# Gate and up projections by seven half-size products (Strassen's scheme) in a tuned trunk layer

## The chip, the cores and the metric

The kernel runs on one core of one Trainium2 chip. Its time is the device time of one execution in microseconds; a kernel is run three times and the median is given. One further execution is recorded by the hardware profiler, and every row below comes from that one.

## The reference, cut to what matters

One inference step of one trunk layer for 512 prompt tokens and 8 sequences of 4 sample tokens, 544 tokens in all, model width 1024. A mixing sub-layer (convolutions, short convolution, dilated attention, an output projection) is followed by a channel sub-layer, a gated MLP of inner width 2816. The part that the change touches is the second one:

```
    h = _rmsnorm(x, lp['g_pre_ffn']) * (1 + sc_f) + sh_f
    g, new_f = _causal_dwconv(h @ lp['w_gate'], st_f, lp['conv_f_w'])
    f = jax.nn.silu(g) * (h @ lp['w_up'])
    x = x + ga_f * _rmsnorm(f @ lp['w_down'], lp['g_post_ffn'])
```

`_causal_dwconv` is a convolution over three tokens for each channel. Everything is float32; `sc_f`, `sh_f` and `ga_f` come from a small projection of a conditioning vector (weights `ada`), one value for the whole prompt and one for each sample sequence.

## The kernel before

Tokens lie on the free axis in two halves of H = 272 (`h` 0 and 1; the sample tokens are the last 32 of half 1), channels on 128 partitions in chunks: the model width is 8 chunks, the inner width 22 blocks of 128. A float32 product is three passes (`mm3`, L231 to L233): weights and activations are each split into a high part that the TensorE takes as fp32r and the low rest, and high·high, high·low and low·high are added up in PSUM. One block of 128 outputs for one half is 8 chunks × 3 passes = 24 matmuls of 272 columns.

Splitting weights is `prep`: ScalarE copies 1024 columns of raw weights into the high part (L227), VectorE or GpSimd subtracts to get the low part (L228). Raw weights come by SyncE's DMA queue into a ring of four slots of 1 MB (`Ring`); a slot is refilled when its last user is done. Split weights go round in three sets of tiles, `st[0..2]` (`sth`/`stl`).

The instructions of each engine stand in the order in which the program's steps are written; engines wait for each other by semaphores. Three pieces of the program matter here.

The string `FLOW` orders the stretch from the out-projection to the first three gate/up pairs. In it `a` and `b` are steps of the chain `post_mix` for half 0 and half 1 (norm, residual, second norm, and `modul`, which makes the MLP's input `z` as `zh`/`zl`); `m` is a gate or up product, `y` and `u` its evaluations `gate_ev` and `up_ev`, `g` a weight split, `d0` to `d3` four steps of the `ada` projection (`adb_step`, L309), `f` their end. A p at the end of a name puts the work on GpSimd, else it is VectorE's.

Then the loop over pairs: for each inner block `j` from 3 to 21 the gate product for both halves, its evaluation (PSUM to SBUF on ScalarE, three taps on VectorE, Silu on ScalarE), the up product for both halves, its evaluation (product with the gate, split of the result `f` into `fh`/`fl` for the down projection), and two weight splits for the next pair:

```
    for j in range(NA, NFF):
        for h in range(2):
            step(lambda j=j, h=h: gu_mm(2 * j, h))
        step(lambda j=j: gate_ev(j, 0))
        gu_or_dn_prep(2 * j + 3)
        step(lambda j=j: gate_ev(j, 1))
```

Then the down projection: units of 8 chunks of its weights, split by `dn_prep` one after the other into the three sets, and `dn_mm`.

The factor of a norm is worked out on few partitions and spread over 128 by `rs_bc`: three matmuls of float32 against the identity for each half (L266).

Of the kernel before, what the change touches and what calls it, by code (L numbers as in the profile page):

```python
# [13 lines left out]
F32 = mybir.dt.float32  # L14
# [6 lines left out]
T = NP + NB * NT  # L21
# [23 lines left out]
         "02 12 P3d2 22 03 H3 A4 31 30 32 Q2p4 H4 13 23 33 A5 40123 H5 A6 A7 501 52 H6 H7 P4d2 53 6012 701 Q4p4 63 "  # L45
         "723")
FLOW = ("p3d w1068 w0068 w2008 e10 w3008 e20 p4d p6p p5d w4008 e00 e40 p7d w5008 e50 w6008 w7008 w7104 e30 e60 e70 "
        "a w7148 e71 a a a a w2108 w1108 a e11 w3108 e21 a w4104 a g0p e31 p0d a w4148 g1p a a a e41 a a w5108 e51 "
        "a w6108 a a a e61 o w0108 g2d e01 m0004 b g3d x m0048 b m1003 d0 g4p b b d1 b b m1038 m2008 b g5d m3008 b "
        "b d2 b b b d3 b b b b b m4008 b y10 y00 m5008 f u10 m0108 g6d m1108 m2107 m2178 y20 u00 g7p y01 u01 u20 "  # L50
        "m4108 m3108 y11 m5108 y21 u11 g8d u21")

_V = {}
_n = 0
# [42 lines left out]
def body(tc, nc, A):  # L97
# [75 lines left out]
    class Ring:  # L173


        def __init__(self):
            self.slots, self.free, self.order, self.pos, self.uses, self.where = {}, [], [], 0, {}, {}

        def setup(self):
            for _, keys in plan:  # L180
# [33 lines left out]
        def done(self, k):  # L214
            self.uses[k] -= 1
            if not self.uses[k]:
                self.free.append(self.where.pop(k))
                self.pump()

    ring = Ring()  # L220

# [5 lines left out]
            act.activation(hi, r[:, a:a + n, :], AF.Copy)  # L227
            eng.tensor_sub(lo, r[:, a:a + n, :], hi.bitcast(F32))  # L228

    def mm3(acc, wh, wl, rh, rl, start, stop):  # L230
        pe.matmul(acc, wh, rh, start=start, stop=False)  # L231
        pe.matmul(acc, wh, rl, start=False, stop=False)  # L232
        pe.matmul(acc, wl, rh, start=False, stop=stop)  # L233

    ALL = tuple(range(NCH))

# [2 lines left out]
        for c in cs:  # L239
            mm3(acc[:, :H], pair[0][:, c, :], pair[1][:, c, :], a[h][:, c, :], b[h][:, c, :], c == first, c == last)  # L240

    BLK = ((0, 128, 0), (128, 128, 0), (256, H - 256, 384 - H))

    def rs_acc(parts, tsum, nh, first, last):

        for j, s in enumerate(parts):
            for h in range(nh):
                for i, o in enumerate((0, 128, H - 128)):
                    pe.matmul(tsum[:, 3 * h + i:3 * h + i + 1], s[:, h * H + o:h * H + o + 128], ones[:, 0:1],  # L249
                              start=first and j == h == i == 0, stop=last and j == len(parts) - 1,  # L250
                              skip_group_check=True)
# [10 lines left out]
    def rs_bc(r, outs):  # L262

        for h, o in enumerate(outs):
            for i, (c0, n, k0) in enumerate(BLK):
                pe.matmul(o[:, c0:c0 + n], r[:, 3 * h + i:3 * h + i + 1].to_broadcast([128, 128]),  # L266
                          idn[:, k0:k0 + n], start=True, stop=True)

    class Banks:

# [647 lines left out]

    Q = {}
    p2r = ExitStack()  # L920
    p2l = ExitStack()
    x2s = ExitStack()

    def open_p2():
        p1.close()
        psc.close()
        p = psc.enter_context(tc.tile_pool(name="psd", bufs=1, space=bass.MemoryType.PSUM))
        Q["sc"] = [p.tile([128, 512], F32, name=f"sc{i}") for i in range(2)]
        x2p = x2s.enter_context(tc.tile_pool(name="x2p", bufs=1, side="right"))
        Q["xh"] = [x2p.tile([128, NCH, H], F32R, name=f"zh{i}") for i in range(2)]  # L930
        Q["xl"] = [x2p.tile([128, NCH, H], F32R, name=f"zl{i}") for i in range(2)]
        xy = p2r.enter_context(tc.tile_pool(name="xyp", bufs=1, side="right"))
        Q["x"] = [xy.tile([128, NCH, H], F32, name=f"x2_{i}") for i in range(2)]
        Q["y"] = [xy.tile([128, NCH, H], F32, name=f"y2_{i}") for i in range(2)]
        Q["tmp"] = xy
        Q["ss"] = [xy.tile([128, 2, H], F32, name=f"ss2_{i}") for i in range(2)]
        Q["rc"] = xy.tile([128, NNEW], F32, name="rc")
        wq = p2l.enter_context(tc.tile_pool(name="p2w", bufs=1))
        Q["w"] = [(wq.tile([128, 8, 128], F32R, name=f"woh{i}"), wq.tile([128, 8, 128], F32R, name=f"wol{i}"))
                  for i in range(4)]  # L940
        for h in range(2):
            pool.dma_start(Q["x"][h], A["x"][:, :, h * H:h * H + H])
        act.activation(Q["rc"][:, 0:1], ones[:, 0:1], AF.Silu)
# [47 lines left out]
    def post_mix(h):  # L991
# [30 lines left out]
        ts_ = {}  # L1022

        def lo(c):
            dve.scalar_tensor_tensor(dl[:, c, :n], ts_.pop(c)[:, :n], sh[:, c, 0:1], dh[:, c, :n].bitcast(F32),
                                     op0=OP.add, op1=OP.subtract)

        def modul(c):
            if c == 0 and h == 1:
# [24 lines left out]
        chains[h].pop(0)()  # L1054

    gu_set = {0: st[2], 1: st[0], 5: st[1]}
    for i in range(6, 2 * NFF):
        gu_set[i] = st[(2, 0, 1)[(i - 6) % 3]]
    dn_set = [st[(2, 0, 1)[(i + 2 * NFF - 6) % 3]] for i in range(64)]

    def gu_prep(i, eng=dve):
        step(lambda: prep(ring.get(("gu", i // 2))[:, (i % 2) * 1024:(i % 2) * 1024 + 1024], gu_set[i], eng),
# [2 lines left out]
    R = {}  # L1065
    p3t = ExitStack()
    p3w = ExitStack()

    def open_p3():
        p2l.close()  # L1070
# [5 lines left out]

    NA = 3

    def f_slices(j, h):
        if j < 8:  # L1080
            return xh[h][:, j, :], xl[h][:, j, :]
        return R["fh"][h][:, j - 8, :], R["fl"][h][:, j - 8, :]


    def gu_mm(i, h, a=0, b=NCH):
        acc = acb.take((i, h)) if a == 0 else bk[acb.of[i, h]]
# [3 lines left out]
        return Q["sc"][1]  # L1090

    def ada_fin():
        adb_end(1, bk_ada(), Q["y"][1][:, 0, :256])
        gain(gqf, 40, "gqf", False)

    G = {}
# [4 lines left out]
    def gate_ev(j, h):  # L1101
# [12 lines left out]
            pool.tensor_copy(fpo[:, j, :], gp[:, NP:])  # L1114
            pool.tensor_copy(fso[:, j, :, :], gs[:, :, NT:])
        n = H if h == 0 else HB
        y = gy()
        G[j, h] = y
        c0 = h * H
        dve.tensor_scalar(y[:, :n], gp[:, c0:c0 + n], V("cfw", 3 * j), None, op0=OP.mult)  # L1120
# [10 lines left out]
    def up_ev(j, h):  # L1131
# [4 lines left out]
        act.activation(fh, y, AF.Copy)  # L1136
        dve.tensor_sub(fl, y, fh.bitcast(F32))

    def close_xy():
        p2r.close()  # L1140
        p3w.close()
        f = p3w.enter_context(tc.tile_pool(name="fp", bufs=1))
        R["fh"] = [f.tile([128, NFF - 8, H], F32R, name=f"fh{i}") for i in range(2)]
        R["fl"] = [f.tile([128, NFF - 8, H], F32R, name=f"fl{i}") for i in range(2)]

    wo_prep(2, pool)
    for fn in late:
# [3 lines left out]
    for w in FLOW.split():  # L1151
        k, i = w[0], [int(c) for c in w[1:] if c.isdigit()]
        eng = pool if w[-1] == "p" else dve
        if k == "p":
            wo_prep(i[0], eng)
        elif k == "w":
            step(lambda i=i: wo_mm(*i))
        elif k == "e":
            step(lambda i=i: wo_ev(*i))
        elif k in "ab":  # L1160
            step(lambda h="ab".index(k): run_chain(h))
        elif k == "g":
            gu_prep(i[0], eng)
        elif k == "m":
            step(lambda i=i: gu_mm(*i))
        elif k == "d":
            s_adc(i[0])
        elif k == "y":
            step(lambda i=i: gate_ev(*i))
        elif k == "u":  # L1170
            step(lambda i=i: up_ev(*i))
        elif k == "f":
            step(ada_fin)
        elif k == "o":
            step(open_p3)
        else:
            step(lambda: ring.add_tiles([Q[k][0].rearrange("p c t -> p (c t)") for k in "xy"], ("adc",)))
    step(close_xy)


# [13 lines left out]
        step(lambda: prep(ring.get(("dn", u // 2))[:, (u % 2) * 1024:(u % 2) * 1024 + 1024], dn_set[i]),  # L1194
             ("dn", u // 2))

    def gu_or_dn_prep(i):
        if i < 2 * NFF:
            gu_prep(i)
        else:  # L1200
            dn_prep(i - 2 * NFF)

    for j in range(NA, NFF):
        for h in range(2):
            step(lambda j=j, h=h: gu_mm(2 * j, h))
        step(lambda j=j: gate_ev(j, 0))
        gu_or_dn_prep(2 * j + 3)
        step(lambda j=j: gate_ev(j, 1))
        for h in range(2):
            step(lambda j=j, h=h: gu_mm(2 * j + 1, h))  # L1210
        step(lambda j=j: up_ev(j, 0))
        gu_or_dn_prep(2 * j + 4)
        step(lambda j=j: up_ev(j, 1))

    def ff_state_out():
        pool.dma_start(A["o_fp"], fpo)
# [2 lines left out]
    step(ff_state_out)  # L1219

    def open_p4():
        x2s.close()
        p = p4.enter_context(tc.tile_pool(name="p4", bufs=1, side="right"))
        S["x"] = [p.tile([128, NCH, H], F32, name=f"x4_{i}") for i in range(2)]
        S["y"] = [p.tile([128, NCH, H], F32, name=f"y4_{i}") for i in range(2)]
        for h in range(2):
            pool.dma_start(S["x"][h], xd[:, :, h * H:h * H + H])
        S["ss"] = [p.tile([128, 2, H], F32, name=f"ss4_{i}", bufs=1) for i in range(2)]
# [8 lines left out]
    def dn_mm(i, u, hs, qs):  # L1237
        for q in qs:
            m, k = MK[q]
            for h in hs:  # L1240
                if k == 0:
                    ACC[m, h] = acb.take((m, h))
                fh, fl = f_slices(k, h)
                mm3(ACC[m, h][:, :H], dn_set[i][0][:, q - 8 * u, :], dn_set[i][1][:, q - 8 * u, :], fh, fl,
                    k == 0, k == NFF - 1)
            if k == NFF - 1:
                for h in hs:
                    acb.give((m, h))
                    post_sq(h, m, m, ACC.pop((m, h)), S["ss"][h], S["y"][h], gqf, gy)

    def gy():
        return R["t"].tile([128, H], F32, name="gy", bufs=3)

    def final(h):

# [39 lines left out]
        for k in keys:  # L1295
            ring.done(k)
    p4.close()
    p3w.close()
    p3t.close()
    psc.close()  # L1300
    ctx.close()


# [102 lines left out]
```

## Time and profile before

| | |
|---|---|
| time, median of 3 runs | 759.72 us (758.55 to 762.98) |
| the profiled execution | 758.35 us, of which its instructions span 756.5 us |
| TensorE (PE) busy | 724.0 us, 96% |
| VectorE (DVE) busy | 438.7 us, 58% |
| ScalarE (ACT) busy | 295.6 us, 39% |
| GpSimd (POOL) busy | 200.3 us, 26% |

Times in the profile count from the first instruction of the span. Busy time is a share over the whole span; the stages below differ from it. A matmul's row shows 0.29 us from issue to end, but matmuls overlap, so the start of one to the start of the next is what a row costs. "Idle before" names what the engine waited for.

### The profile page before, as it was taken

How to read it: one execution, taken by the hardware profiler on the slowest of the kernel's cores; microseconds unless marked ns; L12 is line 12 of the kernel's file. 1: busy time of each engine (PE TensorE's matmuls, PEld its weight loads, DVE VectorE, ACT ScalarE, POOL GpSimd, SP SyncE). 2: the span in 40 equal slices, each digit the busy share in tenths (PEclk: the TensorE clock that was granted, in tenths of full speed). 3: DMA queues.
4: the chain of work that ended last, by engine and by line, in shares of the span. 5: the costliest groups of instructions: out<-in, count | busy, mean ns of one | idle time of the engine just before them, and what ended most of it. 6: DMA issues, size and time to landing. Idle time of an engine off the chain costs nothing.

```text
span 756.5 us, 15327 instructions
## 1 busy us (share of the span) xinstructions
PE 724.0 (96%) x6356; PEld 682.8 (90%) x6356; DVE 438.7 (58%) x879; ACT 295.6 (39%) x632; POOL 200.3 (26%) x254
## 2 busy tenths in 40 slices
PE   8998898979999989989999999999999999999994
PEld 8887776967879789988999999999999999999994
DVE  4869888885354464477767666666556641111343
ACT  4434343635452336553333433333333323222440
POOL 3644232312232255475211011110101110100124
PEclk9999999999999989999999999999999999999997
DMA  9979962766656547058212231312213171220002
GB/s 357 416 265 291 320 253 88 280 236 250 274 221 232 201 163 260 26 186 314 109 66 70 102 113 56 112 63 106 101 68 112 57 240 64 105 71 41 1 29 90
DMA packets 30549, 121.22 MB, mean 160 GB/s; under 512 B 11168, under 2 KB 13488, under 8 KB 21392
## 3 DMA queue, kind: packets, MB, share of 16 engines
q1 hardware_dynamic: 27952, 112.49, 41.0%
q0 software_dynamic: 1808, 7.07, 2.7%
q8 instruction: 50, 0.82, 0.4%
q10 hardware_dynamic: 720, 0.69, 0.3%
q14 instruction: 19, 0.16, 0.1%
HBM read 113.05 MB, written 7.18 MB: 159 GB/s over the span
## 4 chain that ended last, share of the span: by engine, by line
PE 53%; POOL 1%; DVE 1%; ACT 0%; issue 0%; POOLq 0%; DVEq 0%
PE bk L231 17%; PE bk L233 17%; PE bk L232 17%; PE sc L249 1%; PE sc L266 1%; POOL y L1014 0%; DVE y L988 0%; PE sc L309 0%; DVE x L989 0%; POOL y L988 0%; POOL x L989 0%; ACT wgh L227 0%; POOL rr L259 0%; POOLq L1402 0%; DVE y L1014 0%
## 5 line engine op out<-in xcount | busy, mean ns | idle before, releaser
L231 PE MATMUL bk<-zh,sth 128*128 128x272 f32 x656 | 189.6, 289 | 0.0
L233 PE MATMUL bk<-zh,stl 128*128 128x272 f32 x656 | 189.6, 289 | 0.0
L232 PE MATMUL bk<-zl,sth 128*128 128x272 f32 x656 | 188.8, 288 | 0.0
L228 DVE TENSOR_TENSOR stl<-ring,sth 128x1024 fp32r<-128x1024 f32 (+2 forms) x78 | 88.0, 1136 | 152.4 <-ACT sth L227 152.4
L231 PE MATMUL bk<-xh,sth 128*128 128x272 f32 x488 | 146.2, 300 | 2.1 <-DVE q L546 2.1
L233 PE MATMUL bk<-xh,stl 128*128 128x272 f32 x488 | 142.8, 293 | 0.0
L232 PE MATMUL bk<-xl,sth 128*128 128x272 f32 x488 | 142.7, 292 | 0.0
L227 ACT ACTIVATE sth<-ring 128x1024 fp32r<-128x1024 f32 (+3 forms) x104 | 101.9, 991 | 84.9 <-PE bk L232 82.3
L231 PEld LDWEIGHTS bk<-zh,sth 128*128 128x128 f32 x656 | 123.7, 189 | 0.4 <-issue 0.4
L232 PEld LDWEIGHTS bk<-zl,sth 128*128 128x128 f32 x656 | 124.0, 189 | 0.0
L233 PEld LDWEIGHTS bk<-zh,stl 128*128 128x128 f32 x656 | 123.7, 189 | 0.0
L231 PEld LDWEIGHTS bk<-xh,sth 128*128 128x128 f32 x488 | 94.4, 194 | 6.9 <-issue 6.6
L232 PEld LDWEIGHTS bk<-xl,sth 128*128 128x128 f32 x488 | 94.5, 194 | 0.1
L233 PEld LDWEIGHTS bk<-xh,stl 128*128 128x128 f32 x488 | 94.1, 193 | 0.0
L228 POOL TENSOR_TENSOR stl<-ring,sth 128x1024 fp32r<-128x1024 f32 (+1 forms) x26 | 61.6, 2368 | 107.7 <-ACT sth L227 103.6
L1114 POOL COPY fpo<-gp 128x2 f32<-128x2 f32 x22 | 19.3, 879 | 202.3 <-ACT gp L1112 202.3
L231 PE MATMUL bk<-fh,sth 128*128 128x272 f32 x224 | 64.9, 290 | 0.0
L233 PE MATMUL bk<-fh,stl 128*128 128x272 f32 x224 | 64.7, 289 | 0.0
L232 PE MATMUL bk<-fl,sth 128*128 128x272 f32 x224 | 64.4, 287 | 0.0
L741 DVE SCALAR_TENSOR_TENSOR cv<-apad,vec,cv 128x512 f32<-128x512 f32 x60 | 61.9, 1031 | 1.8
L1129 ACT ACTIVATE gy<-gy 128x272 f32<-128x272 f32 x44 | 19.0, 432 | 102.3 <-DVE gy L1128 65.5
L1122 DVE SCALAR_TENSOR_TENSOR gy<-gp,vec,gy 128x272 f32<-128x272 f32 (+1 forms) x88 | 42.7, 485 | 3.1
(243 smaller groups left out, 1217.8 us busy)
## 6 DMA issues: line engine op xcount, KB each, us to landing
ring<-in_w_gu SPq DMA_DIRECT2D x22, 1024.0 KB, 4.9
ring<-in_ada SPq DMA_DIRECT2D x15, 1024.0 KB, 8.3
ring<-in_kc SPq DMA_DIRECT2D x16, 896.0 KB, 6.0
ring<-in_vc SPq DMA_DIRECT2D x16, 896.0 KB, 7.1
ring<-in_w_dn SPq DMA_DIRECT2D x11, 1024.0 KB, 4.9
ring<-in_w_in SPq DMA_DIRECT2D x10, 1024.0 KB, 10.3
ring<-in_ad SPq DMA_DIRECT2D x8, 1024.0 KB, 14.1
ring<-in_w_o SPq DMA_DIRECT2D x4, 1024.0 KB, 8.0
```

The source lines that it names most:

```text
L227: act.activation(hi, r[:, a:a + n, :], AF.Copy)
L228: eng.tensor_sub(lo, r[:, a:a + n, :], hi.bitcast(F32))
L231: pe.matmul(acc, wh, rh, start=start, stop=False)
L232: pe.matmul(acc, wh, rl, start=False, stop=False)
L233: pe.matmul(acc, wl, rh, start=False, stop=stop)
L249: pe.matmul(tsum[:, 3 * h + i:3 * h + i + 1], s[:, h * H + o:h * H + o + 128], ones[:, 0:1], start=first and j == h == i == 0, stop=last a ...
L266: pe.matmul(o[:, c0:c0 + n], r[:, 3 * h + i:3 * h + i + 1].to_broadcast([128, 128]), idn[:, k0:k0 + n], start=True, stop=True)
L741: dve.scalar_tensor_tensor(cv[:, j, :NP], ap_[:, j, k:k + NP], V("caw", j * WA + k), cv[:, j, :NP], op0=OP.mult, op1=OP.add)
L1114: pool.tensor_copy(fpo[:, j, :], gp[:, NP:])
L1122: dve.scalar_tensor_tensor(y[:, :n], gp[:, c0 + k:c0 + k + n], V("cfw", 3 * j + k), y[:, :n], op0=OP.mult, op1=OP.add)
L1129: act.activation(y, y, AF.Silu)
```

## The change

Pairs 0 to 2 stay. For pairs 3 to 21 gate and up of both halves become one product of 2×2 blocks: rows are gate and up, the inner dimension is two groups of four chunks, columns are the two halves. The Winograd form of Strassen's scheme makes it from seven products of four chunks (84 matmuls instead of 96) on sums of blocks. Sums of the weights, S1 to S4, are made by GpSimd for each pair into a ring slot that is held for it (`s_add`, four instructions of 512 columns); sums of `z`, T1 to T4, are made and split once (`t_add`, `t_split`; names A and B in `FLOW`). To have the sums, `modul` also writes `z` itself, by one more ScalarE operation for each chunk (in `lo`). A pair has 3 × 1024 + 512 columns of weights to split, where it had 2 × 1024 (`w_prep`). The seven results are put together by `copy_out` (ScalarE), `c11`, `c12`, `c21` (VectorE, one operand in PSUM), `sum_57`, `c22` (GpSimd); the taps, Silu and the product with the gate then run on 512 or 544 columns at once. `f` is kept as it is for pairs 6 to 21 and split at the end of pair 21 or behind it (`f_split`), into the places of `z` and T. The four `ada` steps go from `FLOW` to pairs 6 to 9. `rs_bc` uses transposes.

```
-            for i, (c0, n, k0) in enumerate(BLK):
-                pe.matmul(o[:, c0:c0 + n], r[:, 3 * h + i:3 * h + i + 1].to_broadcast([128, 128]),
-                          idn[:, k0:k0 + n], start=True, stop=True)
+            for i, c0 in enumerate(BLK):
+                pe.transpose(o[:, c0:c0 + 128], r[:, 3 * h + i:3 * h + i + 1].to_broadcast([128, 128]), idn)
...
+            act.activation(t, t, AF.Identity, bias=sh[:, c, 0:1], scale=1.0)
...
+    def t_add(i, eng):
+        y0, y1 = Q["y"]
+        for a in (0, 2):
...
+            eng.tensor_sub(raw_t(i, a), b, c)
+
+    def t_split(i, eng):
+        h, l = t_(i)
+        for a in (0, 2):
+            act.activation(h[:, a:a + 2, :], raw_t(i, a), AF.Copy)
+            eng.tensor_sub(l[:, a:a + 2, :], raw_t(i, a), h[:, a:a + 2, :].bitcast(F32))
...
+    def s_add(j, pair, eng=pool):
+        w = ring.get(("gu", j))
+        a11, a12, a21, a22 = (w[:, 512 * i:512 * i + 512] for i in range(4))
+        if pair:
+            eng.tensor_sub(s_raw(2), s_raw(1), a11)
+            eng.tensor_sub(s_raw(4), a12, s_raw(2))
+        else:
+            eng.tensor_add(s_raw(1), a21, a22)
+            eng.tensor_sub(s_raw(3), a11, a21)
...
+        if i == 0:
+            prep(ring.get(("gu", j))[:, :1024], st[2], eng)
+        elif i < 3:
+            prep(ring.slots[ring.taken][0][:, 1024 * (i - 1):1024 * i], st[(2, 0, 1)[i]], eng)
+        else:
+            prep(ring.get(("gu", j))[:, 1536:], w_unit(6, j), eng, n=4, last=4)
...
+        do(p_step, j, 1)
+        old_(c21)
+        if old:
+            s_prep(2, j)
+        do(copy_out, j, "a", "p1")
+        if new:
+            s_sums(j + 1, 0)
+        old_(tap0)
+        old_(taps)
+        do(p_step, j, 5)
+        do(copy_out, j, "b", "p5")
+        old_(taps_s)
+        s_prep(3, j)
+        old_(gate)
+        do(p_step, j, 7)
+        do(copy_out, j, "c", "p7")
+        do(sum_57, j)
+        old_(gated)
+        if new:
+            s_prep(1, j + 1)
+        else:
+            dn_prep(0)
+        do(p_step, j, 2)
+        do(c11, j)
+        if new:
+            s_sums(j + 1, 1)
+            s_prep(0, j + 1)
...
+        do(p_step, j, 6)
+        do(copy_out, j, "a", "u2")
+        step(lambda j=j: acb.give(("a", j)))
+        do(c22, j)
...
+    for fn in (c21, tap0, taps, taps_s, gate):
+        do(fn, j)
+    for k in range(NF + 3, NFF - 1):
+        do(f_split, k)
+    do(gated, j)
+    do(f_split, j)
```

Here `p_step(j, i)` is product i of pair j; P1, P5, P7, P2, P6, P3, P4 is their order. P1, P2 and P3 read weights as they come, P5, P7 and P6 read S1, S3 and S2, and P4 reads S4.

VectorE, one pair in the middle of the loop, before: the three taps of half 0 and half 1 (L1120 to L1128), the products with the gate and the splits of f (L1134, L1137), and two weight splits of 1024 columns.

```order
L1120 TENSOR_SCALAR gy<-gp,vec 128x272
L1122 SCALAR_TENSOR_TENSOR gy<-gp,vec,gy 128x272 x2
L228 TENSOR_TENSOR stl_111<-ring_132,sth_110 128x1024
L1120 TENSOR_SCALAR gy<-gp,vec 128x240
L1122 SCALAR_TENSOR_TENSOR gy<-gp,vec,gy 128x240 x2
L1126 TENSOR_SCALAR gy<-gs,vec 128x32
L1128 SCALAR_TENSOR_TENSOR gy<-gs,vec,gy 128x32 x2
L1134 TENSOR_TENSOR gy<-gy,bk_91 128x272
L1137 TENSOR_TENSOR fl_4219<-gy,fh_4217 128x272
L228 TENSOR_TENSOR stl_107<-ring_135,sth_106 128x1024
```

VectorE, one pair in the middle of the loop, now. `stl_107`, `stl_111` and `stl_109` are the low parts of sets 0, 2 and 1, `zl` that of the 512 columns; `ring_135` is the held slot with the sums.

```order
L237 TENSOR_TENSOR stl_107<-ring_135,sth_106 128x1024
L1263 TENSOR_TENSOR gp_4240<-bk_93,p_4235 128x272
L237 TENSOR_TENSOR stl_111<-ring_134,sth_110 128x1024
L1267 TENSOR_TENSOR gp_4240<-bk_95,u_4238 128x240
L1268 TENSOR_TENSOR gs_4242<-bk_95,u_4238 128x8x4
L1271 TENSOR_TENSOR fraw<-bk_96,u_4238 128x272
L237 TENSOR_TENSOR stl_109<-ring_135,sth_108 128x1024
L1286 SCALAR_TENSOR_TENSOR gy_4244<-gp_4240,vec,gy_4244 128x512 x2
L1291 TENSOR_SCALAR gy_4244<-gs_4242,vec 128x32
L1293 SCALAR_TENSOR_TENSOR gy_4244<-gs_4242,vec,gy_4244 128x32 x2
L237 TENSOR_TENSOR zl_3182<-ring_134,zh_3180 128x512
L1305 TENSOR_TENSOR fraw<-fraw,gy_4244 128x544
```

The split of set 2, which the next pair's P1 reads, now stands behind the product with the gate and the split of set 0.

GpSimd, the same pair, now; before it had a memset and three copies of at most 16 columns there (L1107, L1108, L1114, L1115).

```order
L1211 TENSOR_TENSOR ring_135<-ring_133 128x512
L1212 TENSOR_TENSOR ring_135<-ring_133 128x512
L1259 COPY gs_4242<-fst 128x8x2
L1260 TENSOR_TENSOR p_4236<-p_4236,p_4237 128x272
L1208 TENSOR_TENSOR ring_135<-ring_135,ring_133 128x512
L1209 TENSOR_TENSOR ring_135<-ring_133,ring_135 128x512
L1274 TENSOR_TENSOR fraw<-p_4236,u_4238 128x272
L1277 COPY fpo<-gp_4239 128x2
L1278 COPY fso<-gs_4241 128x16
```

L1211 and L1212 make S1 and S3, L1208 and L1209 make S2 and S4, L1260 and L1274 are sums of products. Four instructions of 512 columns and two of 272 are new on this engine.

VectorE between the last pair and the down projection, now. Before, the weight splits of the down projection took the places of those of a next pair, with the taps and splits of pair 21 between them.

```order
L1302 TENSOR_TENSOR zl_3181<-fraw,zh_3179 128x544 x2
L1302 TENSOR_TENSOR xh_103<-fraw,th 128x544 x2
L1302 TENSOR_TENSOR xh_102<-fraw,th 128x544 x2
L1302 TENSOR_TENSOR zl_3182<-fraw,zh_3180 128x544 x2
...
L1302 TENSOR_TENSOR zl_3182<-fraw,zh_3180 128x544
L1305 TENSOR_TENSOR fraw<-fraw,gy_4244 128x544
...
L237 TENSOR_TENSOR stl_109<-ring_134,sth_108 128x1024
L237 TENSOR_TENSOR stl_107<-ring_134,sth_106 128x1024
```

The third weight split of the down projection, into set 1 (`stl_109`), now stands behind twelve splits of f, the last product with the gate and the thirteenth split.

## Rows read from the trace of the kernel before

**Rows 1.** The page: span and busy time.

```profile
span 756.5 us, 15327 instructions
PE 724.0 (96%) x6356; PEld 682.8 (90%) x6356; DVE 438.7 (58%) x879; ACT 295.6 (39%) x632; POOL 200.3 (26%) x254
```

**Rows 2.** Busy time by stage: PE, PEld, DVE, ACT, POOL; clock, DMA share, GB/s.

```profile
333.00:363.00 30.00, 27.21 (x237) 24.77 (x236) 19.93 (x36) 11.99 (x24) 15.98 (x19) 0.94 0.68 248
363.00:381.00 18.00, 18.00 (x145) 18.00 (x144) 12.90 (x28) 6.53 (x16) 3.18 (x5) 1.00 0.17 62
381.00:609.50 228.50, 228.50 (x1826) 228.50 (x1825) 141.00 (x297) 86.12 (x177) 28.95 (x81) 1.00 0.25 88
```

**Rows 3.** VectorE groups by line and shape: busy, mean ns, idle before.

```profile
L228 DVE TENSOR_TENSOR stl<-ring,sth 128x1024 fp32r<-128x1024 f32 x70 | 85.7, 1225 | 152.4 <-ACT sth L227 152.4
L1134 DVE TENSOR_TENSOR gy<-gy,bk 128x272 f32<-128x272 f32 x44 | 18.9, 430 | 0.6 <-ACT gy L1129 0.6
L1128 DVE SCALAR_TENSOR_TENSOR gy<-gs,vec,gy 128x32 f32<-128x32 f32 x44 | 11.1, 252 | 1.6
```

**Rows 4.** Timelines (start, duration, instruction) of VectorE and GpSimd at three places.

```profile
293.04 2.48 POOL L228 TENSOR_TENSOR wol<-ring,woh 128x1024 fp32r<-128x1024 f32 x1 [3.48 <-ACT woh L227]
293.93 2.68 DVE L228 TENSOR_TENSOR wol<-ring,woh 128x1024 fp32r<-128x1024 f32 x1 [0.67 <-ACT woh L227]
...
392.05 1.23 DVE L228 TENSOR_TENSOR stl<-ring,sth 128x1024 fp32r<-128x1024 f32 x1 [1.50 <-ACT sth L227]
392.34 0.99 POOL L1114 COPY fpo<-gp 128x2 f32<-128x2 f32 x1 [8.99 <-ACT gp L1112]
...
379.81 0.20 POOL L1114 COPY fpo<-gp 128x2 f32<-128x2 f32 x1 [4.63 <-ACT gp L1112]
```

**Rows 5.** VectorE, durations of one line: least, median, most; and 544 columns in a timeline.

```profile
L741 DVE SCALAR_TENSOR_TENSOR cv<-apad,vec,cv x44: 729/752/2950, 60.0 to 148.9; 128x512 f32<-128x512 f32 x44
343.18 0.72 DVE L989 TENSOR_TENSOR x<-x,y 128x544 f32<-128x544 f32 x1
```

**Rows 6.** Timeline of TensorE at a norm, and at its L639 transposes.

```profile
321.30 0.74 PE L266 MATMUL sc<-idn,rr 128*128 128x128 f32 x6
321.89 0.37 PE L231 MATMUL bk<-xh,woh 128*128 128x272 f32 x1
...
167.95 0.60 PE L639 MATMUL bk<-idn,e 128*128 128x128 f32 x4
```

**Rows 7.** ScalarE groups by line and shape.

```profile
L227 ACT ACTIVATE sth<-ring 128x1024 fp32r<-128x1024 f32 x93 | 98.0, 1058 | 84.9 <-PE bk L232 82.3 <-POOL x L989 2.4
L1012 ACT ACTIVATE y<-x 128x544 f32<-128x544 f32 x8 | 5.3, 659 | 12.2 <-DVE x L989 6.5 <-POOL wgl L228 5.7
L1038 ACT ACTIVATE zh<-y,mod 128x272 fp32r<-128x272 f32 x8 | 4.1, 522 | 5.5 <-DVE y L1037 5.4
L1038 ACT ACTIVATE zh<-y,mod 128x240 fp32r<-128x240 f32 x8 | 3.8, 492 | 2.5 <-DVE y L1037 2.5
L1109 ACT ACTIVATE gp<-bk 128x272 f32<-128x272 f32 x22 | 8.7, 393 | 1.2 <-PE bk L233 0.3
```

**Rows 8.** Timeline of TensorE around the second norm of half 1, and its stretch of 3.4 us.

```profile
336.07 0.27 PE L249 MATMUL sc<-ones,ss 128*128 128x1 f32 x1 [1.91 <-DVE ss L997]
341.80 1.93 PE L309 MATMUL sc<-ring,ct 128*32 128x256 f32 x32
337.20:340.60 3.40, 3.40 (x18) 0.51 0.36 104
```

**Rows 9.** Timeline of VectorE in the chain of half 1.

```profile
356.25 0.45 DVE L1037 SCALAR_TENSOR_TENSOR y<-x,gffn,sc 128x240 f32<-128x240 f32 x1
...
360.02 0.45 DVE L1037 SCALAR_TENSOR_TENSOR y<-x,gffn,sc 128x240 f32<-128x240 f32 x1
```

**Rows 10.** GpSimd: one line's least, median and most, and one instruction in a timeline.

```profile
L228 POOL TENSOR_TENSOR stl<-ring,sth x26: 1292/2380/3457, 28.2 to 372.5; 128x1024 fp32r<-128x1024 f32 x23, 128x512 fp32r<-128x512 f32 x3
333.83 0.76 POOL L964 TENSOR_TENSOR ss<-ss 128x272 f32<-128x272 f32 x1
```

## What the change will do to the time

> **What bounds the kernel now.** I read the page first: TensorE is busy 96% of the span [rows 1]. A mean hides stages, so I cut the span at the places that the change touches [rows 2]. From 381 to 609.5 us, the loop over pairs 3 to 21, TensorE is busy in every microsecond; that stretch is 19 pairs × 96 = 1824 matmuls, so one costs 228.5 / 1824 = 0.1253 us and a pair 12.03 us. VectorE has 141 of 228.5 us there and GpSimd 29; both wait for others. From 363 to 381 (the half-1 products of pairs 0 to 2) TensorE is full too; from 333 to 363, around the norms of half 1, it is not. So the loop is TensorE's, and fewer matmuls pay as long as nothing else becomes longer than they are. The reader is to see how much the other two have left, and whether they can use it at the same time.
>
> They can't quite. At 293 us VectorE's weight split starts 0.89 us behind GpSimd's; it takes 2.68 us instead of 1.23 and ends 1.09 us behind the end of GpSimd's [rows 3, 4]. At 392 us it is the other way round: GpSimd's copy of two columns starts 0.29 us behind a VectorE split, takes 0.99 us instead of 0.20 and ends with it [rows 4]. So an instruction of VectorE with two inputs in SBUF and one of GpSimd run one after the other; who starts first goes first. VectorE's L741 shows the same: 0.75 in the median, 2.95 at most [rows 5]. By the trace of this kernel, what an instruction that waited does behind the other's end is a little less than its own time (1.09 of 1.23); I take durations less 0.16 us as what one keeps the other out. The L1134 rows, one operand in PSUM, have a mean of 0.430 with nothing of this kind in it [rows 3]; I take those as free of it.
>
> The Trainium skill (page "SBUF — State Buffer", section "SBUF: two separate sides") says that VectorE and GpSimd share a pair of ports as an exclusive lock, held for the whole instruction by whichever starts first. The trace agrees on the order, but the 1.09 us above is less than a whole instruction.
>
> **The change part by part.** My sum goes against the profiled execution, 758.35 us, of which 1.85 lie around the span; it is 1.4 us under the median.
>
> *Norm factors.* The six records of one L266 group take 0.59 us from their start to the next matmul's, and four transposes of L639 0.60 in all, 0.11 apart [rows 6]: three cost 0.33. One call saves 0.26 us; the program has 16, so at most −4.2. I take −3, as some stand in waits.
>
> *`z` of half 1.* Each `modul` step gets one more ScalarE operation of 0.52 or 0.49 us [rows 7]. In half 0, eight of them stand ahead of the squares that the norm of half 1 waits for: TensorE, which waited 1.91 us for that [rows 8], waits up to 8 × 0.52 = 4.2 us longer. In half 1 a chunk takes 2 × 0.49 = 0.98 us of ScalarE where VectorE's two took 0.75 (L1037 five steps apart, [rows 9]): 8 × 0.23 = 1.8. The four `ada` steps of 1.93 us each [rows 8] that stood in these waits are gone from here, so TensorE has less to put into them. 6.0 less what overlaps: +4.5 (bounds 0 and 6).
>
> *From there to pair 3's P6.* Work for which the two engines take turns, durations less 0.16: T sums and splits on VectorE 8 × 0.56 (0.72, [rows 5]), on GpSimd 8 × 1.2 (0.07 over the 1.29 of 512 columns, [rows 10]); S1 to S4 4 × 1.13; three splits 3 × 1.07; taps and f splits of six half blocks about 6.5. Sum 28.3 us. TensorE's work there is 18 us [rows 2] and P1, P5, P7, P2 of pair 3, 48 × 0.1253 = 6.0: 24. So at least +4, and that only if one of the two always runs. They don't: T waits for the last `z`, each split for ScalarE's copy, S1's and S2's splits (G1, G2) stand behind B1 and B4 in VectorE's or ScalarE's queue, and the evaluations that give PSUM banks back stand between them. Following the queues instruction by instruction with these durations I get 41 us, +17.
>
> *A pair.* TensorE: 84 × 0.1253 = 10.53 us, −1.50. The turns: VectorE 3 × 1.07 + 0.53 (512) + 2 × 0.59 (taps) + 3 × 0.09 + 0.57 (gate) = 5.8; GpSimd 4 × 1.13 + 2 × 0.60 + 0.1 = 5.8. Together 11.6 (11.1 if the small ones count for nothing), already over TensorE's 10.53. The loop that they form is longer. Zero is the third matmul of P1, the first that reads set 2's low part. Rest of P1 1.3; to ScalarE 0.1; copy of P1 0.39 [rows 7]; first tap 0.72 (0.52 for 272 columns with a factor, 0.83 ns for each further one by 0.66 for 544 and 1.06 for 1024, [rows 7]); two taps 0.75 each, but S1 and S3 have begun on GpSimd, so 1.04 and 1.63; three taps of 32 columns 0.78; Silu 0.69; copy of P7 0.39, which stands behind Silu; copy of S1/S3's high part 1.06. By then GpSimd, released by P7's copy, has done L1260 and begun S2 about 0.1 us before VectorE could begin the split of set 0: wait 1.16, the split 1.07, then S4, which waited, 1.10, then the split of set 2 1.07; back to TensorE 0.16. Sum 12.7, +0.70 a pair, in which TensorE waits 2.1 us at that third matmul. 18 pairs (4 to 21): +12.6. Pairs 4 and 5 also split f (2 × 0.72 behind the gate), and pairs 6 to 9 carry the `ada` steps, 7.7 us of TensorE, of which the waits take about half: +5.4.
>
> *To the down projection.* The first two units are split in time; they feed 96 matmuls, 12.0 us. The third unit's split (set 1) stands behind: combining of pair 21, itself behind three f splits, 3.3; taps 1.5 and 0.8; Silu 0.7; twelve splits of f at 0.70 behind ScalarE's lead of 0.9, 9.3; gate 0.73; last split's copy 0.66; copy 1.06 and split 1.23. 19.3 us against 12.0: +7 (bounds 5 and 9).
>
> *Clock.* After the 1.91 us idle the next 3.4 us ran at granted clock 0.51, the lower level, 1.2 GHz [rows 8]. The new waits of about 2 us and above give more such stretches; where one falls into P1 it is on the loop. Each costs up to 1.7 us, most fall on matmuls with time to spare: +3 (0 to 10).
>
> Sum: −3 + 4.5 + 17 + 12.6 + 5.4 + 7 + 3 = +46.5; 758.35 + 46.5 = 804.9. I say **805 us**.
>
> **Rivals.**
> *The race goes the other way.* S2 begins only 0.1 us before the split of set 0. If VectorE wins, its split costs no wait of 1.16: pairs 11.6, −0.4 each, −7.7 instead of +12.6: 785 us. For it: 0.1 us is within what single rows vary. Against: nothing between them changes from pair to pair, so it would have to be off for all. A start that is hidden better (+4, the lower bound) gives 792, both 772.
> *Whole instructions keep each other out, or the clock falls in each pair.* With full durations a pair's turns are VectorE 7.4 and GpSimd 6.9: 14.3, +2.3 a pair, 18 × 2.3 = 41 instead of 12.6: 834. With a slow stretch on P1 of each pair, 1.3 × 18 = +23 instead of +3: 825. Against the first: 1.09 of 1.23 us [rows 4]; against the second: P1 is only a part of what a slow stretch can fall on. The page "SBUF — State Buffer" of the Trainium skill, section "SBUF: two separate sides", speaks for the first.
> *Faster.* VectorE has 5.8 us and GpSimd 5.8 in a pair; if the waits don't appear because the two don't keep each other out with these operands (both in the ring slots, say), the loop without its waits (and with 0.43 for combining P2, which stands in it) is 9.7 us, below 10.53, and TensorE sets the pair: 19 × −1.50 = −28.5; the start loses its turns too. −3 + 4.5 − 28.5 + 4 + 7 = −16: 742 us. It decides below 10.6 us a pair with the start as I have it (25.5 us of other losses, over 18 pairs, −1.42 each) or below 11.3 with the start at +4 (12.5, −0.69 each). For it: GpSimd is only 13% busy in the loop now. Against it: [rows 4], where the same kinds of instructions meet. In between lies no change: pairs of about 10.6 to 11 with half of the start's loss.
>
> **How the numbers follow.** The sum as worked out 0.50 (own range 793 to 817), the race or the start better 0.22, slow stretches or whole instructions 0.15, faster 0.08, no change 0.05. A difference within 0.5% (3.8 us) can't be told from none. Faster 0.08, same 0.05, slower 0.87. The range leaves out faster, no change and a third of the uppermost case: 774 to 832.
>
> **What would show it.** Right: pairs 4 to 21 come every 12.7 us (13 to 14 in pairs 4 to 9), TensorE waits about 2 us in each for VectorE's low part of set 2, behind GpSimd's S2 and S4; VectorE's splits have a mean near 1.8 us; pair 3 starts about 12 us late and its P6 waits about 7; TensorE waits in the first unit's third of the down projection for set 1; L266 groups cost 0.33. Wrong: pairs of 10.5 us with TensorE full, GpSimd's 512-column sums at 1.29 us beside VectorE's splits at 1.23. What would make it wrong is the taking of turns: it carries 30 of the 46 us.

## The result, and the profile after

The changed kernel takes 808.33 us (median of 4 runs, 805.33 to 810.4) where the one before takes 759.13 (4 runs beside it): ratio 1.064, 95% interval 1.061 to 1.0671. It is slower by 49 us, and 805 had been forecast. The profiled execution took 808.61 us, its span is 806.7 us.

The page of the changed kernel, the lines that answer to [rows 1], and its shares of the chain that ended last:

```profile
span 806.7 us, 14962 instructions
PE 719.8 (89%) x6080; PEld 668.5 (83%) x6080; DVE 535.7 (66%) x887; ACT 346.6 (43%) x693; POOL 380.9 (47%) x358
PE 22%; POOL 15%; DVE 12%; issue 6%; ACT 4%; POOLq 0%; DVEq 0%; ACTq 0%
```

The same shares of the kernel before:

```profile
PE 53%; POOL 1%; DVE 1%; ACT 0%; issue 0%; POOLq 0%; DVEq 0%
```

TensorE has 19 × 12 = 228 product matmuls less, but is busy only 4 us less, 89% of a longer span; GpSimd's busy time has grown by 181 us and VectorE's by 97. GpSimd and VectorE now stand in the chain.

The matmul rows of both traces can be counted through in the program's order, so the start of each stage can be read from them. Stages in us, each from its first matmul to the next stage's:

| stage | before | after | difference |
|---|---|---|---|
| to the first product on `z` of half 0 | 332.2 | 334.0 | +1.7 |
| to the first on `z` of half 1 | 29.7 | 32.9 | +3.2 |
| to pair 3 | 18.1 | 25.4 | +7.3 |
| pair 3 | 12.0 | 23.6 | +11.6 |
| pairs 4 to 21 | 216.5 | 235.9 | +19.4 |
| first output block of the down projection | 16.6 | 24.5 | +8.0 |
| from there to the last product | 118.6 | 118.2 | −0.5 |

Windows of the changed kernel (columns as in [rows 2]): around half 1's norms, from half 1's first product to pair 3, pair 3, and about ten pairs of the loop.

```profile
333.00:367.10 34.10, 25.00 (x174) 24.37 (x172) 20.58 (x37) 18.51 (x42) 17.13 (x19) 0.90 0.29 95
367.10:392.50 25.40, 20.30 (x145) 19.64 (x145) 20.90 (x30) 8.62 (x19) 13.01 (x12) 0.90 0.00 1
392.50:417.00 24.50, 17.02 (x92) 16.48 (x93) 18.20 (x27) 9.59 (x21) 16.45 (x18) 0.69 0.13 43
525.00:651.00 126.00, 110.95 (x819) 107.65 (x819) 104.57 (x136) 60.30 (x101) 96.33 (x86) 0.96 0.24 81
```

In the loop VectorE has gone from 141 of 228.5 us to 104.6 of 126, GpSimd from 29 of 228.5 to 96 of 126; TensorE, full before, is no longer what the others wait for. What it waits for is in the list of its waits (total, times, longest; only the rows that bear on the change):

```profile
PE bk L242 <- DVE stl L237: 27.7, 18, 3.3
...
PE bk L240 <- ACT p L1256: 6.4, 1, 6.4
PE bk L240 <- DVE gy L1156: 4.4, 2, 3.9
PE sc L258 <- DVE ss L1007: 3.9, 1, 3.9
PE bk L240 <- ACT sth L236: 3.9, 1, 3.9
```

The first row is the loop, but for two short waits: the low part of set 2 at the third matmul of P1, in 16 of the pairs 4 to 21. The second is pair 3's P6, the third two products ahead of it that need a PSUM bank back, the fourth half 1's norm (1.91 before, [rows 8]), the fifth the third weight split of the down projection (another 0.7 us of that is in the first row).

How one pair goes is seen in the chain of waits between 571 and 588 us (start, length, what):

```profile
571.47 1.10 POOL p L1260
572.57 2.22 POOL ring L1208
574.79 0.07 issue
574.86 2.15 POOL ring L1209
577.01 0.74 POOL fraw L1274
...
578.01 1.25 POOL ring L1211
579.26 2.23 POOL ring L1212
581.48 0.61 POOL gs L1259
582.10 2.48 issue
...
584.61 1.11 POOL p L1260
```

From one L1260 to the next are 13.14 us, and all of it is GpSimd's queue: its sums, three of which take 2.2 us where one alone takes 1.29 ([rows 10]; L1211 here, 1.25), and a wait of 2.48 us. The timelines of the engines show what the sums meet and what that wait is:

```profile
572.37 1.28 DVE L237 TENSOR_TENSOR stl<-ring,sth 128x1024 fp32r<-128x1024 f32 x1 [0.44 <-ACT sth L236]
572.53 2.25 POOL L1208 TENSOR_TENSOR ring<-ring,ring 128x512 f32<-128x512 f32 x1
573.93 1.94 DVE L237 TENSOR_TENSOR stl<-ring,sth 128x1024 fp32r<-128x1024 f32 x1
575.92 0.39 PE L242 MATMUL bk<-zh,stl 128*128 128x272 f32 x1 [2.07 <-DVE stl L237]
577.04 1.06 ACT L236 ACTIVATE sth<-ring 128x1024 fp32r<-128x1024 f32 x1 [3.47 <-POOL ring L1209]
578.13 2.20 DVE L237 TENSOR_TENSOR stl<-ring,sth 128x1024 fp32r<-128x1024 f32 x1 [1.50 <-ACT sth L236]
580.26 2.56 DVE L1286 SCALAR_TENSOR_TENSOR gy<-gp,vec,gy 128x512 f32<-128x512 f32 x2
583.58 0.66 ACT L1296 ACTIVATE gy<-gy 128x544 f32<-128x544 f32 x1 [3.62 <-DVE gy L1293]
584.15 0.38 ACT L1256 ACTIVATE p<-bk 128x272 f32<-128x272 f32 x1
```

S2 (572.53) starts 0.16 us behind the split of set 0 and ends 1.13 us behind its end; the split of set 2 (573.93) waits for S2 in turn and ends 1.09 behind it, the same 1.09 as in [rows 4]. When S4 is done, ScalarE copies set 1 (577.04), its split (578.13) waits for S1, the taps behind it on VectorE (580.26) wait for S3, Silu for the taps, and P7's copy, which GpSimd waited for, stands behind Silu on ScalarE. The loop is closed there. TensorE waits 2.07 us here (575.92), but no step of the loop waits for TensorE.

### The profile page after: what moved, and what is told of

It reads as the page before. It is cut to its first block, busy times and chain, and to the rows that moved or that the text cites. A ratio compares the mean times of both kernels' runs of the same rounds, so it can differ in the third digit from the quotient of the medians.

```text
span 806.7 us, 14962 instructions
## 1 busy us (share of the span) xinstructions
PE 719.8 (89%) x6080; PEld 668.5 (83%) x6080; DVE 535.7 (66%) x887; ACT 346.6 (43%) x693; POOL 380.9 (47%) x358
## 4 chain that ended last, share of the span: by engine, by line
PE 22%; POOL 15%; DVE 12%; issue 6%; ACT 4%; POOLq 0%; DVEq 0%; ACTq 0%
PE bk L242 7%; PE bk L240 7%; PE bk L241 7%; DVE stl L237 3%; POOL ring L1208 3%; POOL ring L1209 3%; POOL ring L1212 3%; POOL ring L1211 2%; POOL p L1260 1%; DVE gy L1286 1%; DVE gy L1144 1%; POOL gs L1259 1%; POOL fraw L1274 1%; ACT sth L236 1%; DVE zl L1302 1%
## 5 line engine op out<-in xcount | busy, mean ns | idle before, releaser
L237 DVE TENSOR_TENSOR stl<-ring,sth 128x1024 fp32r<-128x1024 f32 (+2 forms) x97 | 145.5, 1508 | 114.3 <-ACT sth L236 114.3
L242 PE MATMUL bk<-zh,stl 128*128 128x272 f32 x404 | 123.6, 306 | 26.6 <-DVE stl L237 26.6
L240 PE MATMUL bk<-zh,sth 128*128 128x272 f32 x404 | 123.3, 305 | 11.5 <-DVE gy L1156 3.9
L241 PE MATMUL bk<-zl,sth 128*128 128x272 f32 x404 | 121.0, 299 | 0.0
L240 PE MATMUL bk<-th,sth 128*128 128x272 f32 x356 | 106.8, 300 | 6.9 <-ACT p L1256 6.4
L240 PE MATMUL bk<-xh,sth 128*128 128x272 f32 x360 | 110.3, 307 | 2.1 <-DVE q L554 2.1
L242 PE MATMUL bk<-th,stl 128*128 128x272 f32 x356 | 106.0, 298 | 1.0 <-DVE stl L237 1.0
L242 PEld LDWEIGHTS bk<-zh,stl 128*128 128x128 f32 x404 | 81.1, 201 | 30.4 <-DVE stl L237 30.4
L241 PE MATMUL bk<-xh,sth 128*128 128x272 f32 x356 | 105.7, 297 | 0.4 <-DVE xh L1302 0.4
L240 PEld LDWEIGHTS bk<-th,sth 128*128 128x128 f32 x356 | 71.2, 200 | 7.4 <-ACT p L1256 6.7
L240 PEld LDWEIGHTS bk<-xh,sth 128*128 128x128 f32 x360 | 71.5, 199 | 6.8 <-issue 6.6
L242 PEld LDWEIGHTS bk<-th,stl 128*128 128x128 f32 x356 | 70.4, 198 | 1.4 <-DVE stl L237 1.4
L241 PEld LDWEIGHTS bk<-xh,sth 128*128 128x128 f32 x356 | 71.0, 199 | 0.6 <-DVE xh L1302 0.6
```

The source lines that it names most:

```text
L240: pe.matmul(acc, wh, rh, start=start, stop=False, skip_group_check=more)
L241: pe.matmul(acc, wh, rl, start=False, stop=False, skip_group_check=more)
L242: pe.matmul(acc, wl, rh, start=False, stop=stop, skip_group_check=more)
```

## The experiments

**The norm factors alone.** The kernel before, with `rs_bc` as in the change:

```
-                pe.matmul(o[:, c0:c0 + n], r[:, 3 * h + i:3 * h + i + 1].to_broadcast([128, 128]),
-                          idn[:, k0:k0 + n], start=True, stop=True)
+                pe.transpose(o[:, c0:c0 + 128], r[:, 3 * h + i:3 * h + i + 1].to_broadcast([128, 128]), idn)
```

> The kernel before with the norm factors spread by transposes and nothing else. As predicted: 0.26 us less in each of 16 calls, 755 to 757 us, most likely 3 us less than before. Rival: TensorE waits for something else at the norms anyway, no change that can be measured (758 to 760).

Measured: 755.65 us beside 759.53, ratio 0.9956 (0.9942 to 0.9971), 3.3 us by the ratio. A group of three that took 0.59 us to the next matmul's start [rows 6] takes 0.25:

```profile
318.89 0.49 PE L266 MATMUL sc<-idn,rr 128*128 128x128 f32 x3
319.14 0.37 PE L231 MATMUL bk<-xh,woh 128*128 128x272 f32 x1
```

This part of the change pays by itself, if only 0.4%, and with it alone the kernel beats both others.

**No sums of weights in the loop.**

```
-        step(lambda: s_add(j, pair), ("gu", j))
+        step(lambda: None, ("gu", j))
```

> The changed kernel, in which the loop makes no sums of weights for pairs 4 to 21: GpSimd's four instructions of 512 columns are left out, and every pair works on pair 3's sums. If GpSimd and VectorE taking turns is what makes a pair 13.1 us, pairs fall to TensorE's 84 x 0.1253 = 10.5 us and the time to about 808 - 18 x 2.6 = 762 us, with VectorE's splits back at 1.23 us. If the order of the queues (Silu, P7's copy, the splits of sets 0, 1 and 2 in one loop) makes it, or stretches at the lower clock, pairs stay above 12 us and the time above 788.

Measured: 769.01 us (763.0 to 769.64), 39 less. The start of GpSimd's L1277, once a pair, gives a pair's length in every kernel with the loop (count; least, median, most; first and last start): here (592.2 − 507.9) / 8 = 10.54 us, after the change (590.8 − 512.0) / 6 = 13.13. First this kernel, then the changed one:

```profile
L1277 POOL COPY fpo<-gp x9: 186/186/187, 507.9 to 592.2; 128x2 f32<-128x2 f32 x9
```

```profile
L1277 POOL COPY fpo<-gp x7: 182/189/201, 512.0 to 590.8; 128x2 f32<-128x2 f32 x7
```

TensorE is full again and the pair is its 84 matmuls. VectorE's splits fall from a mean of 1.77 us to 1.37, and its taps from 1.21 to 0.75, though nothing was taken from VectorE. First the changed kernel, 525 to 651 us, then the one without sums, 527 to 611:

```profile
L237 DVE TENSOR_TENSOR stl<-ring,sth 128x1024 fp32r<-128x1024 f32 x29 | 51.3, 1768 | 19.0 <-ACT sth L236 19.0
L1286 DVE SCALAR_TENSOR_TENSOR gy<-gp,vec,gy 128x512 f32<-128x512 f32 x20 | 24.3, 1213 | 0.4
L1212 POOL TENSOR_TENSOR ring<-ring 128x512 f32<-128x512 f32 x9 | 20.5, 2279 | 0.0
```

```profile
L237 DVE TENSOR_TENSOR stl<-ring,sth 128x1024 fp32r<-128x1024 f32 x24 | 33.0, 1373 | 3.1 <-ACT sth L236 3.1
L1286 DVE SCALAR_TENSOR_TENSOR gy<-gp,vec,gy 128x512 f32<-128x512 f32 x16 | 12.0, 751 | 8.4 <-ACT gy L1281 8.2
```

So neither the lower clock nor the order of the other work makes the pair long; GpSimd's sums do. Pair 3 is still 22 us long here: the start has its own cause.

The time is 7 us over the forecast of 762. Pairs 4 to 21 take 196.1 us here, 6.6 more than 18 × 10.53: pairs 5 to 9, among which the splits of f and the `ada` steps fall, are longer than 10.53. And even with no sums at all in the loop the kernel stays slower than the one before (ratio 1.0102, 1.0073 to 1.0132): what is lost ahead of the loop and behind it is more than the loop can win.

**The sums on VectorE.** `s_add(j, pair)` in the loop becomes `s_add(j, pair, dve)`.

> The changed kernel with the sums of weights of pairs 4 to 21 made by VectorE in the same places. No turns are left between splits and sums, but VectorE has about 4 x 0.6 us more of its own, some 10.4 us a pair in a row. If the turns are the loss, pairs come to 10.5 to 12.5 us, the time to 764 to 798. If it is the amount of work in the loop whoever does it, pairs stay near 13 and the time near 808.

Measured: 787.62 us (787.31 to 788.04), 20.7 less; pairs of (597.7 − 502.6) / 8 = 11.89 us by the starts of L1277. The same sums in the same places, but made by one engine, cost 1.2 us a pair less. This alone doesn't tell the turns from speed: a sum that meets nothing takes 1.29 us on GpSimd and 0.68 on VectorE. That the turns are gone is seen in the splits, back at 1.25 us; GpSimd's L1260 (1.10 for 0.77) still meets VectorE, and VectorE is busy 114 of 123.3 us. The views, of this kernel:

```profile
L1277 POOL COPY fpo<-gp x9: 186/186/187, 502.6 to 597.7; 128x2 f32<-128x2 f32 x9
```

```profile
L237 DVE TENSOR_TENSOR stl<-ring,sth 128x1024 fp32r<-128x1024 f32 x31 | 38.7, 1247 | 4.8 <-ACT sth L236 4.8
L1212 DVE TENSOR_TENSOR ring<-ring 128x512 f32<-128x512 f32 x10 | 6.8, 680 | 0.0
```

```profile
505.80:629.10 123.30, 112.56 (x879) 110.42 (x879) 114.03 (x188) 64.84 (x106) 24.43 (x51) 1.00 0.26 90
```

Now VectorE is busy 11.0 of a pair's 11.89 us: its own work is nearly all that a pair lasts. The time lies in the range that was given for the turns being the loss; what is left is the amount of work.

**The third split of the down projection early.**

```
+    dn_prep(2)
     for k in range(NF + 3, NFF - 1):
         do(f_split, k)
...
-        dn_prep(i + 2)
+        if i:
+            dn_prep(i + 2)
```

> The changed kernel with the third weight split of the down projection put in front of the taps' end: ahead of the twelve splits of f, the last product with the gate and the thirteenth split. As predicted the first output block of the down projection is 7 to 8 us shorter, 800 to 802 us. Rival: the splits of f, now later, are what TensorE waits for next, and less than 3 us come back (805 to 808).

Measured: 801.76 us (801.0 to 803.47), 6.6 less. The first output block goes from 24.5 to 19.6 us (16.6 before): at its place the gain is 4.9 us, not the 7 to 8 of the forecast, and the rest of the 6.6 is not explained by it; single executions of the changed kernel lie 5 us apart. What TensorE waits for between 645 and 680 us is now the splits of f, 2.5 us:

```profile
PE bk L240 <- ACT th L1301: 1.5, 1, 1.5
PE bk L241 <- DVE xh L1302: 1.0, 1, 1.0
```

**No rewriting of `z`.** `act.activation(t, t, AF.Identity, ...)` in `lo` is taken out.

> The changed kernel without ScalarE's rewriting of z (16 operations in the two chains; the sums T are then made from z without its shift). As predicted half 1's z is ready 4.5 us earlier (bounds 0 and 6) and the time falls to about 804 us. Rival: VectorE's work between there and pair 3 is what sets pair 3's start, and the time stays within 1 us of 808.

Measured: 807.1 us (804.28 to 809.2), ratio 1.0612 (1.0575 to 1.0649): not to be told from the changed kernel's. At its place the gain is there: from half 0's first product to half 1's are 30.4 us instead of 32.9, and instead of 32.9 to 35.7 in the profiled executions of the four runs whose kernels are the changed one's up to there (those without sums, with the sums on VectorE, with the third split early and with set 1 behind the taps). But from half 1's first product to P6 of pair 3 it takes 41.5 us instead of 40.4, and so on down: what comes behind does not wait for `z` alone. The rival holds for the time, the prediction for the place.

**No subtractions for T.** In `t_add`, `eng.tensor_sub(raw_t(i, a), b, c)` becomes `pass`.

> The changed kernel without the eight subtractions that make T1 to T4 (four on VectorE, four on GpSimd; the splits stay and work on what lies there). If the work that VectorE and GpSimd do in turns sets the start of the loop, 4 x 0.56 + 4 x 1.2 = 7 us go, 800 to 804 us. If it is the order in which the evaluations of pairs 0 to 2 stand behind others and give PSUM banks back, less than 2 us go.

Measured: 801.02 us (800.7 to 802.02), 7.3 less. From half 1's first product to P6 of pair 3: 34.8 us instead of 40.4. Eight instructions less, 7 us by the estimate, give back 5.6 at the place and 7.3 in the time, so the rival of the PSUM banks falls. The subtractions stand in both engines' queues and also wait for `z`; how much of the gain is their work and how much their waits is not shown.

**Set 1 behind the taps.** In the loop `s_prep(2, j)` goes from in front of P1's copy to behind `old_(taps_s)`.

> The changed kernel with the split of set 1 moved behind the taps of the pair before, nothing else. The trace after the change shows a loop: S4, split of set 1, taps, Silu, copy of P7, L1260, S2, S4. If that loop makes the 13.1 us, taking the split out of it leaves the turns, about 11.6 us a pair: 781 to 790 us. If it is the sum of VectorE's own work and what GpSimd holds, whatever the order, pairs stay at 12.7 to 13.4 and the time at 800 to 813.

Measured: 807.06 us (804.05 to 811.29), no change that can be told. The first theory fell: the loop is broken, but the pair is still 12.87 us instead of 13.13. The timeline shows which loop took its place, here in VectorE's and ScalarE's rows of one pair:

```profile
598.06 0.39 PE L242 MATMUL bk<-zh,stl 128*128 128x272 f32 x1 [1.50 <-DVE stl L237]
599.67 0.40 ACT L1256 ACTIVATE p<-bk 128x272 f32<-128x272 f32 x1 [5.87 <-PE bk L242]
599.97 0.72 ACT L1281 ACTIVATE gy<-gp,vec 128x512 f32<-128x512 f32 x1
600.72 2.02 DVE L1286 SCALAR_TENSOR_TENSOR gy<-gp,vec,gy 128x512 f32<-128x512 f32 x2 [1.95 <-ACT gy L1281]
603.39 1.22 DVE L237 TENSOR_TENSOR stl<-ring,sth 128x1024 fp32r<-128x1024 f32 x1
605.12 1.30 DVE L1305 TENSOR_TENSOR fraw<-fraw,gy 128x544 f32<-128x544 f32 x1
606.35 2.31 DVE L237 TENSOR_TENSOR stl<-ring,sth 128x1024 fp32r<-128x1024 f32 x1
608.94 1.95 DVE L237 TENSOR_TENSOR stl<-ring,sth 128x1024 fp32r<-128x1024 f32 x1
610.95 0.39 PE L242 MATMUL bk<-zh,stl 128*128 128x272 f32 x1 [1.51 <-DVE stl L237]
```

P1, its copy, the first tap, the taps, Silu, the product with the gate, the split of set 0, the split of set 2, the next P1: the loop of the prediction, 12.89 us from wait to wait, with VectorE waiting for GpSimd in the taps, at L1305 and in two splits.

**All together.** The sums on VectorE, the third split early, T and its splits on VectorE behind the evaluations, and the tap in front of P1's copy:

```
-        "b b b b b b b b b m4008 b y10 y00 m5008 To A1d u10 S0 m0108 B1d G0d m1108 A3p m2107 m2178 A2d y20 u00 B3p "
-        "G1d B2d y01 u01 m4108 A4p u20 m3108 y11 m5108 B4p y21 u11 S1 u21 G2d")
+        "b b b b b b b b b m4008 b y10 y00 m5008 To S0 A1d u10 m0108 S1 G0d m1108 A3d m2107 m2178 y20 u00 A2d "
+        "G1d y01 u01 A4d m4108 B1d u20 m3108 y11 m5108 B3d y21 u11 G2d u21 B2d B4d")
...
         do(p_step, j, 1)
         old_(c21)
+        old_(tap0)
+        old_(taps)
         do(copy_out, j, "a", "p1")
         if new:
             s_sums(j + 1, 0)
+        old_(taps_s)
+        if old:
+            s_prep(2, j)
         do(p_step, j, 5)
         do(copy_out, j, "b", "p5")
+        old_(gate)
         s_prep(3, j)
```

> All that helped or should: sums of weights on VectorE, the third split of the down projection early, the first tap and the taps in front of P1's copy and of the split of set 1, and T and its splits all on VectorE behind the evaluations of pairs 0 to 2. By the parts 808 - 20.7 - 6.6 = 780.7 us, a few less by the order: 772 to 782. If VectorE's own work (some 10.4 us a pair) and waits of GpSimd's two sums are the bound, pairs stay above 11 us and the kernel stays slower than the one before; faster than before only with pairs below 10.6.

Measured: 780.85 us (779.04 to 781.99), ratio 1.0272 (1.0242 to 1.0301). That is the two gains added; the new orders brought nothing. A pair is (595.5 − 512.1) / 7 = 11.91 us with VectorE busy 114 of 120 us:

```profile
500.00:620.00 120.00, 108.40 (x845) 106.14 (x844) 113.99 (x184) 61.41 (x101) 25.54 (x52) 1.00 0.25 89
```

```profile
L1277 POOL COPY fpo<-gp x8: 186/187/188, 512.1 to 595.5; 128x2 f32<-128x2 f32 x8
```

A pair of seven products thus costs, at the best that was found, what a pair of eight costs without sums (12.03), and the start is paid on top: from half 1's first product to P6 of pair 3 38.3 us instead of 24.1.

## Why the prediction was right, and where it was not

*The taking of turns.* Right, and it carries the result. Without the sums a pair is 10.54 us; with them on GpSimd 13.13; with them on VectorE 11.89. The rival that ended faster needed the two engines not to keep each other out with operands in the ring slots; S2 and the splits of sets 0 and 2, all in the ring, do (572.37 to 575.87 above). By the Trainium skill (page "SBUF — State Buffer", section "SBUF: two separate sides") a VectorE instruction with two inputs in SBUF and a GpSimd instruction that reads SBUF exclude each other: the one that starts first has the shared ports for its whole duration. The trace agrees in who waits, and not quite in how long: behind the other's end an instruction of 1.23 us takes 1.09 and one of 1.29 takes 1.13. The rival by whole instructions, 14.3 us a pair, was not reached.

*A pair, 12.7 us.* The length is nearly right (13.13), the path to it is the step that failed. The prediction had S2 win against the split of set 0 by 0.1 us; VectorE won by 0.16. The rival to that said 11.6 us then, and that was wrong as well: another loop, through S4, set 1's split, the taps, Silu and P7's copy, was 13.14 us long. With that loop cut the predicted one came to light at 12.87. So two loops of nearly one length stood side by side, both made of the two engines' work, and the prediction had counted one of them through.

*Pairs 4 to 9, +5.4.* Too much. The splits of f, in three pairs and not two, make three intervals of 14.15 us instead of 13.14, about 3 us. The `ada` steps went into TensorE's waits: the intervals that hold them are 13.1 to 13.2 us like the rest. Where TensorE is full, in the loop without sums, a step costs 1.2 us (11.74 a pair instead of 10.53), not the 1.93 of the prediction. With +1.1 a pair where +0.70 stood, the two errors nearly cancel: +18.0 forecast, +19.4 measured. That is luck.

*The start, +17.* From half 1's first product to P6 40.4 us instead of 24.1, +16.3; the "41 us" of the text. Leaving eight of the shared instructions out, 7 us by the prediction's durations, made this stretch 5.6 us shorter.

*`z` of half 1, +4.5.* The mechanism is right, and so is the size as far as it can be told: +3.2 at its place in the changed kernel's profile, +3.2 to +6.0 in the four runs named above. But taken out it is worth no more than can be told from nothing: what comes behind takes the gain back, most likely the shared work of the start, which was not tested by itself. The term should have been counted inside the start.

*Norm factors, −3.* −3.3 alone. In the profiled execution of the change it can't be seen: the stretch ahead of `z` took 334.0 us there and 330.8 to 333.7 in the six other kernels that are the same up to that point.

*The down projection, +7.* +8.0, but not by the wait alone. The prediction had TensorE wait 19.3 − 12.0 = 7.3 us for the third split; it waited 4.6 for it (3.9 and 0.7) and 0.8 for splits of f. Behind the long wait 14 matmuls came 0.23 us apart instead of 0.125, at granted clock 0.50 (second row below), some 1.4 us. With the split early the block is 4.9 us shorter. The term came out near its size by what the clock added.

*Clock, +3.* Behind the wait of 6.4 us the 36 matmuls from P6 to the end of pair 3 took 8.6 us, 4.5 at full speed and 1.0 of another wait. That leaves 3.1 us; the granted clock of that stretch was 0.58 (first row):

```profile
407.30:416.00 8.70, 7.47 (x36) 7.15 (x37) 7.61 (x7) 3.52 (x7) 8.62 (x6) 0.58 0.35 122
671.00:673.80 2.80, 2.80 (x13) 2.80 (x13) 1.93 (x2) 0.30 (x1) 0.31 (x1) 0.50 0.89 291
```

With the 1.4 us behind the third split's wait that makes about 4.5 us at two places. In the loop the mean is 0.96, but there TensorE lies beside the path. How much of the loop's time it costs was not measured by itself; with the sums on VectorE the clock was 1.00.

*The sum.* 46.5 us were forecast and 49.2 measured. The two large terms, the loop and the start, came out near their sizes, and the rest is closer than its parts deserve: the errors above have both signs.

Open: whether a start spread over several ordinary pairs, where VectorE has a third of its time free, would make the scheme pay. It wasn't tried; by the pairs of 11.9 us it could gain little.

## What to carry to other kernels

Before a product is traded for sums, add up for the stage what each engine that makes the sums already does, and add VectorE's and GpSimd's work with two operands in SBUF as if it were one engine's: that sum, not the share of busy time, shows the room there is. It is a lower bound: 11.6 us here by the prediction, where the loops made 13.13 of it. Where a pair's work goes round through four engines, look for the second longest loop too; cutting the longest one here gave nothing that can be told. Work that was saved ahead of a stage full of shared work was not seen again in the time. And count what a change costs once, ahead of its loop and behind it: here the kernel with no sums in the loop at all was still 1% slower than the one before.

## What was not expected of the hardware

GpSimd's copy of 16 columns (L1259), 0.20 us in the kernel without sums, took 0.66 to 0.67 behind a tap of VectorE in every pair of the changed kernel but the last; so even tiny GpSimd copies wait. And which of two instructions that start within 0.2 us of each other goes first decides about 1 us. For pairs 8 to 21 the split of set 0 started just ahead of S2, and S2 took 2.24 to 2.31 us. For pairs 5 to 7 a split of f stood in its place and started 0.12 to 0.14 us behind S2: there S2 took 1.29 to 1.31 and the split of f 1.75 instead of 0.72.
